# Differential attention: queries and keys reach the array's rows by transfers through DRAM instead of by products

## The chip, the cores and the metric

The kernel runs on one core of one Trainium2 chip. The metric is device microseconds of one execution, the median of several runs. Five engines work beside each other: PE (TensorE; its weight loads are listed apart as PEld), DVE (VectorE), ACT (ScalarE), POOL (GpSimd), and SP, which here only issues transfers. Sixteen DMA engines move the data.

## The reference

Two layers of a diffusion backbone run over 256 latent tokens and 128 context tokens, d_model 1024. In each layer one projection w_in feeds three groups of heads: A, latent attention (MLA), 6 heads; B, neighbourhood attention, 6 heads; C, differential attention, 4 heads. The heads are joined, projected by w_out, and a SwiGLU feed-forward part follows. The change concerns group C. For each of its heads, cut to what matters:

```python
q_df = _rms_pairs(_heads(df_q, 4), g_df_q)      # 2 x 32 numbers per head and token
k_df = _rms_pairs(_heads(df_k, 4), g_df_k)
q_df = _rope_pairs(q_df, cos, sin)              # latent tokens only
k_df = _rope_pairs(k_df, cos, sin)
s1 = q[..., :32] @ k1.T * 32 ** -0.5            # keys: cached context, then latent
s2 = q[..., 32:] @ k2.T * 32 ** -0.5
p = softmax(s1) - lam * softmax(s2)
o = rms(p @ v, g_df_sub) * (1 - lam_init)
```

## The kernel before, in words

All 384 tokens are kept as three blocks of 128 (t = 0, 1 latent, t = 2 context). Products that need float32 exactness are made from a rounded high part and a low remainder: `mm3` (lines 357 to 359) adds three products hi x hi, hi x lo and lo x hi. Weights come by SP into a `raw` tile (lines 275, 312, 398 for w_mod), ACT rounds them (`wh`, line 285), DVE subtracts (`wl`, line 291).

For group C the same exactness is had in one product. A query of 32 numbers and a key of 32 numbers are spread over the 128 rows of the array, as four groups of 32 rows: the queries as high, low, low, high and the keys as high, high, low, low. One product of 128 rows then sums all four pairings. The tile of a head for that, `du[h]`, has two parts: `du[h][0]` (named `qu`) with the queries of all tokens for both maps, and `du[h][1]` (named `ku`) with the cached keys in front (columns 0 to 127) and the new keys behind.

The work of a layer's attention stage is a list of tasks (`add(engine, planned duration, function, after=..., take=..., frees=..., prio=...)`). A planner (class `Plan`) orders them once at build time: it runs a small model of the engines with the planned durations and priorities, tries 300 drawn variations of the priorities, and keeps the best. The order that it gives is each engine's program order, fixed; at run time an engine waits in it. Projections of w_in (`g1`), early w_out products and the w_mod products (line 408) stand in this list with low priority, between the heads' small steps. `take` names a buffer of a kind that must be free (`ROOM` tells how many there are).

The steps of group C before the change:

- `done_d(p)` for head pair p and block t: copy out of PSUM, mean square, root (POOL, lines 577 and 578), scaling, rotation into `dfo[p][:, t]` (tokens on partitions; 4 groups of query numbers, then 4 of keys). Block 2's keys are stored (line 1327).
- `df_unit(h)`: `fetch` (line 1351) brings the cached keys into `tok` by four transfers of 32 rows; `high` (ACT, line 1354) and `low` (DVE, line 1358) make their parts in `ku`. Then for each block t: `parts_hi` (ACT, lines 1371 and 1372) rounds the head's queries and keys into a `tok` tile, each twice; `parts_lo` (POOL, line 1377) makes the remainders; `stack` (PE, line 1384) multiplies four 128x128 arrangements of them with the identity `identr`, which transposes and spreads them at once; `queries` (ACT, line 1387) and `keys` (DVE, line 1390) copy the result from PSUM into `qu` and `ku`.
- `diff_step(h, t)`: scores (PE, line 1078), softmax, transposes of the probabilities (line 1045), output products (line 1425).

The other names in the rows below: line 1181 is the output product of a pair of heads of A or B, line 935 and 1255 are transposes of A and B, `bias` (line 1137) are B's bias tables, `vn` are B's values, `brief` a small work tile, `out_newc` the new caches that the kernel returns.

Of the kernel before, what the change touches and what calls it, by code (L numbers as in the profile page):

```python
# [12 lines left out]
F32 = mybir.dt.float32  # L13
F32R = mybir.dt.float32r
# [4 lines left out]
P = 128  # L19
DM = 1024  # L20
KD = DM // P
NT = 384
# [39 lines left out]
ROOM = {'z': 3, 's': 2, 't': 2, 'raw': 3, 'graw': 2, 'w': 3, 'tok': 4, 'brief': 2, 'row': 5, 'un': 3, 'e': 4, 'pT': 3, 'pd': 2, 'bias': 2}  # L62
# [151 lines left out]
def trunk(ctx: ExitStack, tc, xT_d, cv_d, crow_d, pcol_d, prow_d, cache_d, dfk_d, rope_d, bias_d, ident_d,  # L214
# [10 lines left out]
    ps_m = ctx.enter_context(tc.tile_pool(name="ps_m", bufs=1, space=PSUM))  # L225

    cnt = [0]

    def nm(s):
        cnt[0] += 1  # L230
        return f"{s}_{cnt[0]}"
# [31 lines left out]
    identr = cst.tile([P, P], F32R, name="identr")  # L263
# [390 lines left out]
    for l in range(DEPTH):  # L654
# [86 lines left out]
        if l == 0:  # L741
            nst = {}
            add(ACT, 0.25, lambda: nc.scalar.activation(sv[:, :, 0:2], cv, AF.Silu), ready=5.0, prio=2 * URGENT)
            add(ACT, 0.2, lambda: nc.scalar.activation(identr, ident, AF.Copy), ready=20.0)
# [538 lines left out]
        dfo, vd, df_ready, vd_ready = {}, [], [{}, {}], [[], []]  # L1283

        def done_d(p):
            hd = slice(2 * p, 2 * p + 2)

            def done(t, z, unit, room):
# [18 lines left out]
                def rotate():  # L1307
                    if p not in dfo:
                        dfo[p] = ws.tile([P, 3, 8, 32], F32, name=nm("dfo"))
                    n, o = (v.rearrange("p (i h) d -> p i h d", i=2) for v in (heads(x["n"], 8), dfo[p][:, t]))  # L1310
# [3 lines left out]
                    if t < 2:  # L1314
# [8 lines left out]
                        nc.vector.tensor_tensor(dfo[p][:, t], dfo[p][:, t], tmp, op=ALU.add)  # L1323
                    else:
                        nc.vector.tensor_tensor(o, n, each(prow[:, PR_DQ:PR_DQ + 64].rearrange("p (i d) -> p i d", i=2)), op=ALU.mult)
                    if t == 2:
                        nc.sync.dma_start(new_d[l, :, CA_DFK + P * p:CA_DFK + P * p + P], dfo[p][:, t, 4:8, :].rearrange("p h d -> p (h d)"))
# [9 lines left out]
                df_ready[p][t] = add(DVE, 1.35 if t < 2 else 0.42, rotate, after=[e], frees=[a], prio=pr)  # L1337
# [4 lines left out]
        def df_unit(h, after, pr):  # L1342


            y = {}

            def fetch():
                du[h] = units(2, P, F32R)
                y["kc"] = tok(256).rearrange("p (a t) -> p a t", a=2)
                for i in range(4):  # L1350
                    nc.sync.dma_start(y["kc"][32 * i:32 * i + 32], dfk_d[l, :, 2 * h:2 * h + 2, :])

            def high():
                nc.scalar.activation(du[h][1][:, :, 0:P], y["kc"], AF.Copy)

            def low():
                kd = du[h][1]
                nc.vector.tensor_tensor(kd[64:, :, 0:P], y["kc"][64:], kd[64:, :, 0:P].bitcast(F32), op=ALU.subtract)
            a = add(DMA, 0.5, fetch, after=after, take=("tok",), prio=pr)
            b = add(ACT, 0.31, high, after=[a], prio=pr)  # L1360
            out = [add(DVE, 0.34, low, after=[b], frees=[a], prio=pr)]
            for t in range(3):
                x = {}

                def parts_hi(t=t, x=x):
                    src = dfo[h // 2][:, t].rearrange("p (i a) d -> p i a d", i=2)[:, :, 2 * (h % 2):2 * (h % 2) + 2, :]
                    both = tok(576, F32R)
                    x["st"] = [v.rearrange("p (a s d) -> p a s d", a=2, d=32) for v in (both[:, :320], both[:, 320:])]
                    x["sb"] = [src[:, i].unsqueeze(2).to_broadcast([P, 2, 2, 32]) for i in range(2)]
                    for i in range(2):  # L1370
                        nc.scalar.activation(x["st"][i][:, :, 0:2, :], x["sb"][i], AF.Copy)
                    nc.scalar.activation(x["st"][0][:, :, 4, :], src[:, 0], AF.Copy)

                def parts_lo(x=x):
                    for i in range(2):
                        st = x["st"][i]
                        nc.gpsimd.tensor_tensor(st[:, :, 2:4, :], x["sb"][i], st[:, :, 0:2, :].bitcast(F32), op=ALU.subtract)

                def stack(tag, x=x):
                    x["pt"] = pt = acc(tag).rearrange("p (i a t) -> p i a t", i=2, a=2)  # L1380
                    for i in range(2):
                        for a in range(2):
                            w = x["st"][i][:, a, 1 - i:5 - i, :].rearrange("p s d -> p (s d)")
                            nc.tensor.matmul(pt[:, i, a, :], w, identr, start=True, stop=True)

                def queries(t=t, x=x):
                    nc.scalar.activation(du[h][0][:, :, t * P:(t + 1) * P], x["pt"][:, 0], AF.Copy)

                def keys(t=t, x=x):
                    nc.vector.tensor_copy(du[h][1][:, :, KEY0[t]:KEY0[t] + P], x["pt"][:, 1])  # L1390
                c = add(ACT, 0.56, parts_hi, after=[a, df_ready[h // 2][t]], take=("tok",), prio=pr)
                d = add(POOL, 0.98, parts_lo, after=[c], prio=pr)
                e = add(PE, 0.47, stack, after=[d], take=("t",), frees=[c], prio=pr)
                out.append(add(ACT, 0.27, queries, after=[e], frees=[e], prio=pr))
                out.append(add(DVE, 0.34, keys, after=[e], frees=[e], prio=pr))
            return out

# [409 lines left out]
```

## Time and profile before

| what | value |
|---|---|
| median of 3 runs | 1011.09 us (1009.39 to 1011.51) |
| profiled execution | 1011.29 us, its span 1009.5 us, clock 0.998 |
| attention stage of layer 0 | about 60 to 215 us of the span |
| attention stage of layer 1 | about 545 to 700 us |
| weights and caches read | 159.69 MB from HBM; 3.05 MB written |

The span runs from the first to the last instruction of the profiled execution. Rows of PE give matmuls whose ends are modelled; rows of PEld give the weight loads, which overlap them. A row of a group lists line, engine, operation, tiles (written <- read), shape, count, then busy time, mean ns of one, and the idle time of the engine just before with what ended it. Lines 357 to 359 with `z` are projections.

### The profile page before, as it was taken

How to read it: one execution, taken by the hardware profiler on the slowest of the kernel's cores; microseconds unless marked ns; L12 is line 12 of the kernel's file. 1: busy time of each engine (PE TensorE's matmuls, PEld its weight loads, DVE VectorE, ACT ScalarE, POOL GpSimd, SP SyncE). 2: the span in 40 equal slices, each digit the busy share in tenths (PEclk: the TensorE clock that was granted, in tenths of full speed). 3: DMA queues.
4: the chain of work that ended last, by engine and by line, in shares of the span. 5: the costliest groups of instructions: out<-in, count | busy, mean ns of one | idle time of the engine just before them, and what ended most of it. 6: DMA issues, size and time to landing. Idle time of an engine off the chain costs nothing.

```text
span 1009.5 us, 16623 instructions
## 1 busy us (share of the span) xinstructions
PE 995.5 (99%) x6074; PEld 929.6 (92%) x6074; DVE 721.8 (71%) x1637; ACT 512.6 (51%) x1206; POOL 174.4 (17%) x263
## 2 busy tenths in 40 slices
PE   9999999999999999999999999999999999999998
PEld 8877778899999999999978878888999999999998
DVE  4678778887999999964356887788889655554342
ACT  3466778765433333333326778796553433333221
POOL 2166123201000000100015633240010000000000
PEclk9999999999999999999999999999999999999999
DMA  9865643327575757684462143322574525244451
GB/s 361 329 200 180 193 135 125 108 87 255 186 242 186 240 181 225 188 278 136 126 216 96 48 152 90 106 89 82 195 243 148 165 88 163 85 127 123 131 146 37
DMA packets 128209, 163.82 MB, mean 162 GB/s; under 512 B 5120, under 2 KB 107136, under 8 KB 125824
## 3 DMA queue, kind: packets, MB, share of 16 engines
q1 hardware_dynamic: 119712, 134.33, 41.5%
q0 software_dynamic: 6832, 27.77, 7.9%
q8 instruction: 48, 0.79, 0.3%
q10 hardware_dynamic: 1584, 0.66, 0.2%
q14 instruction: 33, 0.27, 0.1%
HBM read 159.69 MB, written 3.05 MB: 161 GB/s over the span
## 4 chain that ended last, share of the span: by engine, by line
PE 89%; ACT 5%; DVE 2%; POOL 1%; DMA 1%; issue 1%; ACTq 0%; DVEq 0%; POOLq 0%
PE z L357 13%; PE z L359 13%; PE z L358 13%; PE t L358 6%; PE t L357 6%; PE t L359 6%; PE s L357 5%; PE s L358 5%; PE s L359 5%; PE s L1078 4%; PE t L1045 2%; PE m L408 2%; PE t L1181 1%; PE s L952 1%; PE s L750 1%
## 5 line engine op out<-in xcount | busy, mean ns | idle before, releaser
L285 ACT ACTIVATE wh<-raw 128x768 fp32r<-128x768 f32 (+3 forms) x224 | 203.5, 909 | 365.4 <-PE z L358 138.1
L291 DVE TENSOR_TENSOR wl<-raw,wh 128x768 fp32r<-128x768 f32 (+3 forms) x224 | 231.8, 1035 | 112.5 <-ACT wh L285 110.9
L357 PE MATMUL z<-fh,wh 128*128 128x386 f32 x304 | 103.2, 339 | 0.0
L358 PE MATMUL z<-fl,wh 128*128 128x386 f32 x304 | 103.1, 339 | 0.0
L357 PE MATMUL z<-wh,hh 128*128 128x384 f32 (+1 forms) x264 | 101.3, 384 | 1.8 <-ACT hh L550 1.4
L359 PE MATMUL z<-fh,wl 128*128 128x386 f32 x304 | 102.6, 338 | 0.0
L480 DVE CUSTOM_DVE_ANT_0 sums<-wt,sums,pcol 128x1024 f32<-128x1024 f32 x80 | 102.3, 1278 | 0.3 <-ACT sums L469 0.3
L359 PE MATMUL z<-wh,hl 128*128 128x384 f32 (+1 forms) x264 | 90.5, 343 | 0.5 <-DVE hl L558 0.5
L358 PE MATMUL z<-wl,hh 128*128 128x384 f32 (+1 forms) x264 | 90.0, 341 | 0.0
L578 POOL TENSOR_TENSOR small<-small,mhalf 128x4 f32<-128x4 f32 (+4 forms) x58 | 75.5, 1302 | 4.8
L357 PE MATMUL s<-fh,wh 128*128 128x386 f32 x200 | 68.2, 341 | 0.0
L357 PE MATMUL t<-fh,wh 128*128 128x386 f32 x200 | 68.1, 340 | 0.0
L358 PE MATMUL t<-fl,wh 128*128 128x386 f32 x200 | 67.8, 339 | 0.0
L358 PE MATMUL s<-fl,wh 128*128 128x386 f32 x200 | 67.7, 339 | 0.0
L359 PE MATMUL s<-fh,wl 128*128 128x386 f32 x200 | 67.5, 338 | 0.0
L359 PE MATMUL t<-fh,wl 128*128 128x386 f32 x200 | 67.5, 338 | 0.0
L1101 ACT ACTIVATE e<-s,small 128x384 f32<-128x384 f32 (+1 forms) x114 | 57.8, 513 | 15.2 <-DVE small L1090 9.0
L474 POOL DMA_DIRECT2D wt<-in_w_modT x40 | 21.5, 539 | 252.4 <-DVE mod L480 186.5
L357 PEld LDWEIGHTS z<-wh,hh 128*128 128x128 f32 x264 | 50.0, 189 | 11.0 <-issue 4.6
L358 PEld LDWEIGHTS z<-fl,wh 128*128 128x128 f32 x304 | 57.5, 189 | 0.0
L359 PEld LDWEIGHTS z<-fh,wl 128*128 128x128 f32 x304 | 57.3, 189 | 0.0
L357 PEld LDWEIGHTS z<-fh,wh 128*128 128x128 f32 x304 | 57.2, 188 | 0.0
(299 smaller groups left out, 2414.4 us busy)
## 6 DMA issues: line engine op xcount, KB each, us to landing
raw<-in_w_gate SPq DMA_DIRECT2D x22, 1024.0 KB, 6.2
raw<-in_w_up SPq DMA_DIRECT2D x22, 1024.0 KB, 5.4
raw<-in_w_down SPq DMA_DIRECT2D x32, 704.0 KB, 4.7
wt<-in_w_modT POOLq DMA_DIRECT2D x40, 512.0 KB, 4.1
raw<-in_w_mod SPq DMA_DIRECT2D x16, 1024.0 KB, 5.1
raw<-in_w_in SPq DMA_DIRECT2D x40, 384.0 KB, 4.0
raw<-in_w_out SPq DMA_DIRECT2D x8, 640.0 KB, 4.4
qu<-in_w_mod SPq DMA_DIRECT2D x8, 512.0 KB, 8.5
```

Of the source, the lines that this page charges most:

```text
L285: nc.scalar.activation(hi, src, AF.Copy)
L291: nc.vector.tensor_tensor(lo, src, hi.bitcast(F32), op=ALU.subtract)
L357: nc.tensor.matmul(out, sh, mh, start=first, stop=False)
L358: nc.tensor.matmul(out, sh, ml, start=False, stop=False)
L359: nc.tensor.matmul(out, sl, mh, start=False, stop=last)
L408: nc.tensor.matmul(self.pm[32 * g:32 * g + 32, :n], sv[:, kb + k, :], w[g // self.per][:, k, i * n:(i + 1) * n], start=(kb + k == 0), stop ...
L474: nc.gpsimd.dma_start(self.w[:, self.loaded % 3], w_modT[l, c * P:(c + 1) * P])
L480: nc.vector.tensor_tensor_reduce(self.junk, self.w[:, self.n % 3], self.s[:, v], 1.0, pcol[l][:, PC_BMOD + c:PC_BMOD + c + 1], ALU.mult, A ...
L578: nc.gpsimd.tensor_tensor(out, t[:, :n], mhalf[:, :n], op=ALU.pow)
L1045: nc.tensor.transpose(pt[:, b, :], x, ident)
L1078: nc.tensor.matmul(ps[:, i, :], q, k, start=True, stop=True)
L1101: nc.scalar.activation(x["e"][i], ps[:, j, :], AF.Exp, bias=x["mx"][:, i:i + 1], scale=-1.0 if bias else 1.0, accum_out=x["su"][:, i:i + 1])
```

## The change

`done_d` goes further than before. After the rotation, which now writes a tile `dfo` of one pair and block, the four query groups (128 columns) and the four key groups (128 columns) are each transposed once (`turn`, two transposes on PE). `high` (ACT) rounds the transposed 128x256 from PSUM into a tile `hs`, `low` (DVE) subtracts to get the remainders, and `away` writes both, 128 partitions x 512 numbers, to a tile in DRAM, `parts_d[p]`, of which block t is a third. `df_unit(h)` no longer has `parts_hi`, `parts_lo`, `stack`, `queries` and `keys`. It keeps the cached keys as they were, and a step `spread` issues eight transfers on SP, four for the queries and four for the keys: each reads the high or the low part of one head, 2 x 32 rows of 384 tokens, from DRAM and writes it to 32 rows of `qu` or `ku`. It comes after the `fetch` of the head and after the stores of all three blocks of its pair. The planner's durations are 0.7 (`away`) and 2.3 (`spread`), and transfers get its usual 2.8 on top until their data count as there.

```diff
-ROOM = {..., 'pd': 2, 'bias': 2}
+ROOM = {..., 'pd': 2, 'bias': 2, 'dfo': 2, 'hs': 2}
...
+        parts_d = [dram.tile([P, 2, 2, NT], F32, tag=f"parts{p}", name=nm("parts")) for p in range(2)]
...
-                    if p not in dfo:
-                        dfo[p] = ws.tile([P, 3, 8, 32], F32, name=nm("dfo"))
+                    x["o"] = wk.tile([P, 8, 32], F32, tag="dfo", name=nm("dfo"), bufs=ROOM["dfo"])
...
+                def turn(tag):
+                    x["pt"] = acc(tag)[:, :256].rearrange("p (i t) -> p i t", i=2)
+                    for i in range(2):
+                        nc.tensor.transpose(x["pt"][:, i, :], x["o"][:, 4 * i:4 * i + 4, :].rearrange("p h d -> p (h d)"), ident)
+
+                def high():
+                    x["hs"] = wk.tile([P, 2, 2, P], F32R, tag="hs", name=nm("hs"), bufs=ROOM["hs"])
+                    nc.scalar.activation(x["hs"][:, 0], x["pt"], AF.Copy)
+
+                def low():
+                    nc.vector.tensor_tensor(x["hs"][:, 1], x["pt"], x["hs"][:, 0].bitcast(F32), op=ALU.subtract)
+
+                def away():
+                    nc.sync.dma_start(parts_d[p][:, :, :, t * P:(t + 1) * P], x["hs"].bitcast(F32))
...
-                df_ready[p][t] = add(DVE, 1.35 if t < 2 else 0.42, rotate, after=[e], frees=[a], prio=pr)
+                f = add(DVE, 1.35 if t < 2 else 0.42, rotate, after=[e], take=("dfo",), frees=[a], prio=pr)
+                if t == 2:
+                    add(DMA, 0.3, store, after=[f], frees=[f], prio=pr)
+                g = add(PE, 0.23, turn, after=[f], take=("t",), frees=[f], prio=pr)
+                u = add(ACT, 0.3, high, after=[g], take=("hs",), frees=[g], prio=pr)
+                v = add(DVE, 0.33, low, after=[u], frees=[g], prio=pr)
+                df_ready[p][t] = add(DMA, 0.7, away, after=[v], frees=[u], prio=pr)
...
+            def spread():
+                src = parts_d[h // 2][64 * (h % 2):64 * (h % 2) + 64]
+                for i, order in enumerate(((0, 1, 1, 0), (0, 0, 1, 1))):
+                    for j, w in enumerate(order):
+                        nc.sync.dma_start(du[h][i][32 * j:32 * j + 32, :, (0, P)[i]:(0, P)[i] + NT].bitcast(F32),
+                                          src[:, w, i].rearrange("(a r) t -> r a t", a=2))
...
-                c = add(ACT, 0.56, parts_hi, after=[a, df_ready[h // 2][t]], take=("tok",), prio=pr)
-                d = add(POOL, 0.98, parts_lo, after=[c], prio=pr)
-                e = add(PE, 0.47, stack, after=[d], take=("t",), frees=[c], prio=pr)
-                out.append(add(ACT, 0.27, queries, after=[e], frees=[e], prio=pr))
-                out.append(add(DVE, 0.34, keys, after=[e], frees=[e], prio=pr))
+            c = add(DVE, 0.34, low, after=[b], frees=[a], prio=pr)
+            d = add(DMA, 2.3, spread, after=[a] + [df_ready[h // 2][t] for t in range(3)], prio=pr)
+            return [c, d]
```

The planner orders the new list anew. Three places in layer 0 show what moved (the changed kernel's line numbers are up to 3 lower; 1333 is `turn`, 1337 the new `high`, 1343 `away`, 1373 `fetch`, 1387 `spread`).

First, PE where the last scores of the third MLA pair are done and head 1 is made ready. Before (1384 is the stack, 1714 the tiles of a pair of B, `z` a projection):

```order
L1078 MATMUL s_1892<-ku_640,qu_639 128x384
L1078 MATMUL s_1897<-ku_640,qu_639 128x128 x2
L1045 MATMUL t_1902<-ident,e_1846 128x128 x3
L1045 MATMUL t_1915<-ident,e_1880 128x128 x3
L408 MATMUL m_1699<-raw_1729,sv 32x256 x8
L1384 MATMUL t_1936<-identr,tok_1830 128x128 x4
L1045 MATMUL t_1947<-ident,e_1920 128x128 x3
L1078 MATMUL s_1952<-ku_1714,qu_1713 128x384
L1384 MATMUL t_1960<-identr,tok_1867 128x128 x4
```

Now, from the same last scores on:

```order
L1077 MATMUL s_1920<-ku_661,qu_660 128x128 x2
L1044 MATMUL t_1925<-ident,e_1874 128x128 x3
L1180 MATMUL t_1931<-pT_1560,vm_133 64x256
L1180 MATMUL t_1931<-pT_1613,vm_133 64x256
...
L357 MATMUL z_1734<-wh_1798,hh_120 128x384
L358 MATMUL z_1734<-wl_1815,hh_120 128x384
L359 MATMUL z_1734<-wh_1798,hl_121 128x384
L1077 MATMUL s_2105<-ku_1946,qu_1945 128x384
L1077 MATMUL s_2107<-ku_1946,qu_1945 128x384
```

The stacks are gone, and head 1's first two scores (`ku_1946`, `qu_1945`) stand 46 rows behind the last MLA score, with no PE work for the head itself between.

Second, SP at the same place. Before (the four `tok` transfers are head 1's cached keys):

```order
L1219 DMA ku_1714<-in_cache 128x3x128
L398 DMA raw_1729<-in_w_mod 128x2x1024
L1250 DMA out_newc<-brief_1850 128x128
L1351 DMA tok_1908<-in_dfk 32x256 x4
L398 DMA raw_1945<-in_w_mod 128x2x1024
L1137 DMA bias_1997<-in_bias 128x640
```

Now:

```order
L312 DMA raw_1860<-in_w_in 128x768 x2
L398 DMA raw_1895<-in_w_mod 128x2x1024
L1373 DMA tok_1947<-in_dfk 32x256 x4
L1387 DMA qu_1945<-parts_136 32x2x384 x4
L1387 DMA ku_1946<-parts_136 32x2x384 x4
L1136 DMA bias_2034<-in_bias 128x640
```

Behind the four transfers of the cached keys stand the eight of `spread`; the bias tables and the next w_mod load come behind them.

Third, PE where a pair's blocks are turned, some 160 rows ahead of head 0's first score. This piece is new:

```order
L1333 MATMUL t_942<-ident,dfo_903 128x128 x2
L408 MATMUL m_703<-raw_846,sv 32x512 x4
L951 MATMUL s_961<-qu_512,ku_513 128x288 x2
L934 MATMUL t_968<-ident,tok_820 96x128 x3
L994 MATMUL s_975<-ku_513,ckT_130 128x384
L934 MATMUL t_980<-ident,tok_820 96x128 x3
L951 MATMUL s_988<-qu_512,ku_513 128x288 x2
L951 MATMUL s_1009<-qu_512,ku_513 128x288 x2
L1333 MATMUL t_1019<-ident,dfo_1007 128x128 x2
```

The turns of blocks 1 and 2 stand among MLA's own products, in the time in which before no C work stood on PE.

More of the change, by code (lines that the diff above doesn't have):

```diff
@@ L61 @@
 HOPS = {('pe', 'act'): 0.22, ('pe', 'dve'): 0.22, ('act', 'pe'): 0.22, ('dve', 'pe'): 0.27, ('pool', 'dve'): 0.18, ('dve', 'pool'): 0.18, ('act', 'dve'): 0.15, ('dve', 'act'): 0.13}
-ROOM = {'z': 3, 's': 2, 't': 2, 'raw': 3, 'graw': 2, 'w': 3, 'tok': 4, 'brief': 2, 'row': 5, 'un': 3, 'e': 4, 'pT': 3, 'pd': 2, 'bias': 2}
+ROOM = {'z': 3, 's': 2, 't': 2, 'raw': 3, 'graw': 2, 'w': 3, 'tok': 4, 'brief': 2, 'row': 5, 'un': 3, 'e': 4, 'pT': 3, 'pd': 2, 'bias': 2, 'dfo': 2, 'hs': 2}
 CHUNKS = (((0, 416),),) + tuple(tuple((c + 128 * p, 128) for c in (1568, 1824, 2080)) for p in range(2)) + tuple(
@@ L225, in trunk @@
     ps_m = ctx.enter_context(tc.tile_pool(name="ps_m", bufs=1, space=PSUM))
+    dram = ctx.enter_context(tc.tile_pool(name="dram", bufs=1, space=bass.MemoryType.DRAM))
     cnt = [0]
@@ L262, in trunk @@
     nc.gpsimd.dma_start(ident, ident_d)
-    identr = cst.tile([P, P], F32R, name="identr")
     rope = cst.tile([P, 2, 2, 32], F32, name="rope")
@@ L743, in trunk @@
             add(ACT, 0.25, lambda: nc.scalar.activation(sv[:, :, 0:2], cv, AF.Silu), ready=5.0, prio=2 * URGENT)
-            add(ACT, 0.2, lambda: nc.scalar.activation(identr, ident, AF.Copy), ready=20.0)
             def idle(n, *tag):
@@ L1280, in done_n @@
             return done
-        dfo, vd, df_ready, vd_ready = {}, [], [{}, {}], [[], []]
+        vd, df_ready, vd_ready = [], [{}, {}], [[], []]
+        parts_d = [dram.tile([P, 2, 2, NT], F32, tag=f"parts{p}", name=nm("parts")) for p in range(2)]
         def done_d(p):
@@ L1307, in rotate @@
                 def rotate():
-                    if p not in dfo:
-                        dfo[p] = ws.tile([P, 3, 8, 32], F32, name=nm("dfo"))
-                    n, o = (v.rearrange("p (i h) d -> p i h d", i=2) for v in (heads(x["n"], 8), dfo[p][:, t]))
+                    x["o"] = wk.tile([P, 8, 32], F32, tag="dfo", name=nm("dfo"), bufs=ROOM["dfo"])
+                    n, o = (v.rearrange("p (i h) d -> p i h d", i=2) for v in (heads(x["n"], 8), x["o"]))
                     def each(g):
@@ L1322, in rotate, with store @@
                                                         c4[:, :, s, :].unsqueeze(1).to_broadcast([P, 4, 2, 8]), op=ALU.mult)
-                        nc.vector.tensor_tensor(dfo[p][:, t], dfo[p][:, t], tmp, op=ALU.add)
+                        nc.vector.tensor_tensor(x["o"], x["o"], tmp, op=ALU.add)
                     else:
                         nc.vector.tensor_tensor(o, n, each(prow[:, PR_DQ:PR_DQ + 64].rearrange("p (i d) -> p i d", i=2)), op=ALU.mult)
-                    if t == 2:
-                        nc.sync.dma_start(new_d[l, :, CA_DFK + P * p:CA_DFK + P * p + P], dfo[p][:, t, 4:8, :].rearrange("p h d -> p (h d)"))
+                def store():
+                    nc.sync.dma_start(new_d[l, :, CA_DFK + P * p:CA_DFK + P * p + P], x["o"][:, 4:8, :].rearrange("p h d -> p (h d)"))
+                def turn(tag):
[9 more added lines that the diff above has]
+                    nc.sync.dma_start(parts_d[p][:, :, :, t * P:(t + 1) * P], x["hs"].bitcast(F32))
                 pr = PDD
@@ L1359, in df_unit @@
             a = add(DMA, 0.5, fetch, after=after, take=("tok",), prio=pr)
             b = add(ACT, 0.31, high, after=[a], prio=pr)
[L1361 to L1390, printed above, removed]
-                c = add(ACT, 0.56, parts_hi, after=[a, df_ready[h // 2][t]], take=("tok",), prio=pr)
-                d = add(POOL, 0.98, parts_lo, after=[c], prio=pr)
-                e = add(PE, 0.47, stack, after=[d], take=("t",), frees=[c], prio=pr)
-                out.append(add(ACT, 0.27, queries, after=[e], frees=[e], prio=pr))
-                out.append(add(DVE, 0.34, keys, after=[e], frees=[e], prio=pr))
@@ L1396, in df_unit @@
-            return out
+            c = add(DVE, 0.34, low, after=[b], frees=[a], prio=pr)
+            d = add(DMA, 2.3, spread, after=[a] + [df_ready[h // 2][t] for t in range(3)], prio=pr)
+            return [c, d]
         dn = {}
```

## The prediction

> **What bounds the kernel now.** I read the page first: the busy shares and the chain that ended last.
>
> ```profile
> span 1009.5 us, 16623 instructions
> PE 995.5 (99%) x6074; PEld 929.6 (92%) x6074; DVE 721.8 (71%) x1637; ACT 512.6 (51%) x1206; POOL 174.4 (17%) x263
> ...
> PE 89%; ACT 5%; DVE 2%; POOL 1%; DMA 1%; issue 1%; ACTq 0%; DVEq 0%; POOLq 0%
> ```
>
> PE is busy nearly throughout and carries 89% of the chain. That is a mean over stages, so I cut the span into the two attention stages (60 to 215 us in layer 0, 545 to 700 us in layer 1), where every edited instruction lies, and the feed-forward stages behind them.
>
> ```profile
> core 0: us, PE busy (x) PEld busy (x) DVE busy (x) ACT busy (x) POOL busy (x), PEclk, DMA share, GB/s
> 60.00:215.00 155.00, 152.18 (x988) 123.12 (x989) 124.31 (x354) 113.63 (x357) 56.20 (x78) 1.00 0.43 139
> 215.00:518.00 303.00, 303.00 (x1727) 301.65 (x1726) 238.48 (x450) 121.94 (x188) 22.08 (x39) 1.00 0.62 200
> 545.00:700.00 155.00, 152.63 (x951) 131.68 (x951) 127.97 (x354) 120.49 (x379) 61.47 (x86) 1.00 0.31 98
> ```
>
> In the attention stages PE is idle for 155 - 152.18 = 2.8 us and 155 - 152.63 = 2.4 us, DVE for some 30 us, ACT for some 38 us, and the DMA engines work less than half of the time. The projections of w_in, and behind them those of w_out, stand between the heads as filler. So PE work that is taken out here should shorten the stage by nearly its own time. Only what a new wait costs has to come off.
>
> **The change, part by part.** *PE.* Removed are the stacks: 4 heads x 3 blocks x 4 products = 48 in each layer, 24 groups of four in all. Added are 3 blocks x 2 head pairs = 6 turns in each layer, 12 in all, of two 128x128 transposes each. A stack, a pair of transposes and the score behind them stand one after the other in the timeline of the weight loads:
>
> ```profile
> 137.94 0.52 PEld L1384 LDWEIGHTS t<-identr,tok 128*128 128x128 f32 x4 [0.61 <-issue]
> 138.41 0.20 PEld L1045 LDWEIGHTS t<-ident,e 128*128 128x128 f32 x2
> 138.58 0.30 PEld L1078 LDWEIGHTS s<-ku,qu 128*128 128x128 f32 x2
> ```
>
> From start to start the four products take 138.41 - 137.94 = 0.47 us, and to the end of their loads 0.52 us. Two transposes take 138.58 - 138.41 = 0.17 us, or 0.20 us to the end. I take 0.50 and 0.20 us: 24 x 0.50 = 12.0 us go and 12 x 0.20 = 2.4 us come, a net 9.6 us. The bounds are 24 x 0.47 - 12 x 0.22 = 8.6 us (a turn somewhat longer than the row) and 24 x 0.52 - 12 x 0.17 = 10.4 us. All of it lies in stages where PE is the bound, so all of it is on the path.
>
> *ACT, DVE, POOL.* The groups of the first attention stage, layer 1 being the same within 2%:
>
> ```profile
> L1377 POOL TENSOR_TENSOR tok<-dfo,tok 128x128 fp32r<-128x128 f32 x24 | 12.2, 536 | 5.3 <-ACT tok L1371 5.3
> L1371 ACT ACTIVATE tok<-dfo 128x128 fp32r<-128x128 f32 x24 | 6.1, 304 | 0.8 <-POOL tok L1377 0.8
> L1390 DVE CAST ku<-t 128x256 fp32r<-128x256 f32 x12 | 5.1, 421 | 2.4 <-ACT qu L1387 1.4 <-PE t L1384 0.8
> L1387 ACT ACTIVATE qu<-t 128x256 fp32r<-128x256 f32 x12 | 4.6, 381 | 2.2 <-PE t L1384 1.6 <-DVE ku L1390 0.4
> L1372 ACT ACTIVATE tok<-dfo 128x64 fp32r<-128x64 f32 x12 | 3.0, 248 | 0.0
> L1358 DVE TENSOR_TENSOR ku<-tok,ku 64x256 fp32r<-64x256 f32 x4 | 1.7, 424 | 0.1
> ```
>
> ACT loses 6.1 + 3.0 + 4.6 = 13.7 us in each layer and gains six roundings of 128x256 out of PSUM, priced by L1387: 6 x 0.38 = 2.3 us. DVE loses 5.1 us and gains six subtractions, nearest in form to L1358: 6 x 0.42 = 2.5 us. POOL loses 12.2 us and gains nothing. None of these engines is the bound (table above), so I cost and credit them at nothing; PE's own work is the cover. What their relief could give at most is PE's idle time, 2.8 + 2.4 = 5.2 us. The rounding of the identity that is dropped runs once and on an idle ACT: nothing.
>
> *Transfers.* Each turn's parts go to DRAM in one transfer of 128 x 2 KB = 256 KB, six in a layer. Each head then reads eight pieces of 32 rows x 2 x 384 floats = 96 KB, 32 in a layer, 3.1 MB. Together that is 4.7 MB in each layer beside 139 GB/s x 155 us = 21.5 MB; the DMA share goes from 0.43 to about 0.52, so bandwidth is no bound. The trace has no such piece. Its neighbours, of the same stage:
>
> ```profile
> raw<-in_w_in SPq DMA_DIRECT2D x10, 384.0 KB, 3.8
> bias<-in_bias SPq DMA_DIRECT2D x4, 320.0 KB, 3.0
> tok<-in_dfk SPq DMA_DIRECT2D x16, 32.0 KB, 3.8
> out_newc<-dfo SPq DMA_DIRECT2D x2, 64.0 KB, 1.6
> ```
>
> ```profile
> L1351 SPq DMA_DIRECT2D tok<-in_dfk x32: 326/417/1250, 81.9 to 655.4; - x32
> DMA to landing us min/median/max: 1.6/2.3/4.9
> ```
>
> A store of 256 KB lands after something between the 1.6 us of a 64 KB store and the 3.8 us of a 384 KB load; I take 2.5 us. The pieces are nearest to the four in_dfk pieces, which also write 32 rows each: 0.42 us to issue, 1.6 to 4.9 us to land. From the moment a head's tiles are free, SP issues 4 pieces of in_dfk and 8 of the parts: 12 x 0.42 = 5.0 us, and the last lands 1.6 to 4.9 us later: 6.6 to 9.9 us. I take 7.3, with the median of 2.3. The 38 new issues of a layer cost SP 38 x 0.42 = 16 us of 155.
>
> *What hides that.* The least cover I find in the order is that of head 1 in layer 0. Its tiles come free with the last MLA score of 128 columns (L1077 s_1920 in the order), and its own first score stands 46 rows behind. Between lie two pair outputs, four scores of 384 columns, a w_mod group, 18 projection products and 20 transposes. Prices from the chain, and from 303.00 us over 1727 products in the second row of the table of stages (0.175 us each):
>
> ```profile
> 137.30 0.65 PE s L1078 x2
> ...
> 143.64 1.45 PE t L1181 x12
> ...
> 146.19 1.00 PE m L408 x16
> ```
>
> 2 x 1.45 + 4 x 0.65 + 1.00 + 18 x 0.175 + 20 x 0.10 = 11.7 us of cover against 6.6 to 9.9. In layer 1 head 0's score stands behind a good 20 us of such rows after its last turn. So I cost the waits at 0 to 2 us in all, the value taken 0.5 us, because cover exceeds even the slow landing. If a head is late, the projections behind its score on PE stand with it, since PE's queue is in order.
>
> *Sum.* The profiled execution took 1011.3 us (span 1009.5 and 1.8 around it), 0.2 above the median of 1011.1. 1011.3 - 9.6 + 0.5 = 1002.2; against the median 1002.0.
>
> [...]
>
> **Rivals.** *The stages are paced by the softmax chains, not by PE.* For it: ACT and DVE hold 7% of the whole chain though PE is called 99% busy, and PE's loads leave 32 and 23 us of the two stages open. Against it: the idle rows of PE, and the filler. If half of the removed work only turns into idle PE, the time is 1011.1 - 4.8 = 1006.3. If all of it does, the time stays at 1011.
>
> *More is gained than PE's work.* In layer 0 the first stack waits for POOL:
>
> ```profile
> POOL tok L1377 <- ACT tok L1371: 30.8, 9, 8.0
> ...
> 93.17 1.29 POOL tok L1377 x2
> ```
>
> The chain passes through that subtraction (second row) before the first stacks. With it gone, and ACT relieved of 11 us in each layer, up to the 5.2 us of PE's idle time could go too: 1011.1 - 9.6 - 2.6 = 998.9 with half of it.
>
> *Slower: head-of-line blocking on SP.* The chain of a head begins on SP behind weight loads that stand until a buffer is split:
>
> ```profile
> SPq L312 <- DVE wl L291: 27.9, 7, 6.0
> ```
>
> In layer 0 a w_mod load stands directly ahead of head 1's transfers, in layer 1 w_in loads stand ahead of two heads. If such a wait of 6.0 us falls between the freeing of a head's tiles and its transfers, 7.3 + 6.0 = 13.3 us meet a cover of 11.7, and with the slow landing 15.9, so PE stands for 1.6 to 4.2 us. It takes more than 9.6 + 2.0 = 11.6 us over the eight heads to be slower, 1.5 us on each. At a mean of 1.6 us on each, 12.8 us, the time is 1011.1 + 3.2 = 1014. Against it: the wait of 6.0 us is the longest of seven, and the other heads have more cover. *That the stacks stay* is excluded: the order has no row of them left.
>
> **How the numbers follow.** The full PE gain with small waits (about 1002; 999.8 to 1004.5): 0.60. Half of it eaten by chains or late transfers (about 1006; 1004.5 to 1009): 0.19. More than PE's work (996.5 to 999.8): 0.10. Gain wholly turned to waits, within 0.2% (2 us, about what a measurement can tell from no change): 0.04. Slower: 0.07. So faster 0.89, same 0.04, slower 0.07. The range leaves out the slower and unchanged cases and the outer half of the other two: 998 to 1008.
>
> **What the profile after would show.** PE with some 48 - 12 = 36 fewer instructions in each stage and each stage shorter by 4 to 5 us; POOL's row 24 us smaller and ACT's 23 us; no idle time of PE or PEld before the scores L1077 that ends with a DMA into qu or ku; pieces of parts landing within 5 us. I am wrong if PE idles in front of a head's first score, if SP waits for the store of the parts with weight loads behind it that ACT then waits for, or if the stages shrink by less than 3 us while PE's idle time grows.

## The result and the profile after

| | median | range, runs |
|---|---|---|
| before, beside it | 1011.34 us | 1009.39 to 1014.73, 6 |
| after | 1003.92 us | 999.48 to 1005.07, 6 |
| ratio | 0.9917 | 95%: 0.9898 to 0.9935 |

The ratio is worth 8.4 us (6.6 to 10.3). The forecast was 1002.0, within 998 to 1008. The profiled execution of the changed kernel took 1003.3 us. Its page and its stages, in the rows that were shown of before, with the first 60 us added; the columns are again the width of the stage, busy time and count of PE, PEld, DVE, ACT and POOL, the granted clock, the DMA share and GB/s:

```profile
span 1001.5 us, 16414 instructions
PE 987.9 (99%) x6002; PEld 921.1 (92%) x6002; DVE 711.6 (71%) x1625; ACT 495.8 (50%) x1121; POOL 150.6 (15%) x215
...
PE 79%; DVE 1%; ACT 0%; issue 0%; POOL 0%; DVEq 0%
```

```profile
0.00:60.00 60.00, 54.36 (x507) 47.38 (x508) 30.67 (x102) 23.30 (x55) 14.55 (x24) 0.91 0.85 311
60.00:215.00 155.00, 153.40 (x984) 122.69 (x984) 122.61 (x355) 110.18 (x335) 48.15 (x60) 1.00 0.57 176
545.00:700.00 155.00, 154.92 (x957) 134.01 (x956) 126.20 (x357) 115.51 (x346) 46.22 (x62) 1.00 0.42 128
```

PE makes 72 products fewer (6074 to 6002), and POOL's row is 23.8 us smaller. The chain can't be set beside that of before: its shares add up to 80%, since it goes back only to 187 us of the span, and most of layer 0's attention lies ahead of that. PE's idle time in the two attention stages went from 2.8 and 2.4 us to 155 - 153.40 = 1.6 and 155 - 154.92 = 0.1 us. The surprise is the first row: in the first 60 us, where the change has no instruction, PE is idle for 5.6 us and its clock is 0.91 on average. The same 60 us of before, with 2.2 us of idle time and the full clock:

```profile
0.00:60.00 60.00, 57.83 (x546) 50.68 (x546) 34.58 (x110) 29.35 (x77) 14.80 (x31) 1.00 0.88 329
```

How the gain lies in the two layers is read from two marks in PE's timeline: the start of the first product that makes MLA's keys (line 995, after 994), and the start of the first feed-forward product behind the attention stage (`z<-fh,wh`). Before, then after:

```profile
55.73 0.81 PE L995 MATMUL s<-ku,ckT 128*128 128x384 f32 x2
...
235.42 0.34 PE L357 MATMUL z<-fh,wh 128*128 128x386 f32 x1
...
537.22 2.54 PE L995 MATMUL s<-ku,ckT 128*128 128x384 f32 x4
724.74 0.33 PE L357 MATMUL z<-fh,wh 128*128 128x386 f32 x1
```

```profile
59.44 1.46 PE L994 MATMUL s<-ku,ckT 128*128 128x384 f32 x4
236.70 0.34 PE L357 MATMUL z<-fh,wh 128*128 128x386 f32 x1
...
537.26 1.53 PE L994 MATMUL s<-ku,ckT 128*128 128x384 f32 x4 [0.71 <-PE z L359]
716.45 0.34 PE L357 MATMUL z<-fh,wh 128*128 128x386 f32 x1
```

Layer 0's attention, from mark to mark, took 179.7 us before and takes 177.3 now, 2.4 less, and the first mark is reached 3.7 us later: at 236.7 us the changed kernel is behind. Layer 1's took 187.5 and takes 179.2, 8.3 less. The forecast had 4 to 5 us in each.

The marks don't bound the same work in layer 0. Ahead of the first one PE made 520 products before and makes 505 now: 12 projections of 416 columns and 3 transposes have moved behind it. At 0.19 us from one such projection to the next in the kernel before, and 0.10 us for a transpose, I estimate them at 2.6 us. For the same work layer 0's stage is thus some 5 us shorter, as forecast, and its start some 6 us longer. In layer 1 nothing but the change crossed the marks (1125 products, now 1089); some 1 us of its 8.3 is the clock, which in before was 0.50 from 536.0 to 539.4 us, so that the four products at the mark took 2.54 us against 1.53. All this is read from one execution of each kernel, and l0_only below, with the same order in layer 0, took 179.5 us from mark to mark: the split is good to some 2 us.

That left four questions: what layer 0 lost at its start, whether PE's products are the price at all or the relief of ACT, DVE and POOL, whether the transfers are really covered, and what the new order does by itself.

### The profile page after: what moved, and what is told of

The parts are those of the page before. It is cut to its first block, busy times and chain, and to the rows that moved or that the text cites. A ratio compares the mean times of both kernels' runs of the same rounds, so it can differ in the third digit from the quotient of the medians.

```text
span 1001.5 us, 16414 instructions
## 1 busy us (share of the span) xinstructions
PE 987.9 (99%) x6002; PEld 921.1 (92%) x6002; DVE 711.6 (71%) x1625; ACT 495.8 (50%) x1121; POOL 150.6 (15%) x215
## 4 chain that ended last, share of the span: by engine, by line
PE 79%; DVE 1%; ACT 0%; issue 0%; POOL 0%; DVEq 0%
PE z L357 12%; PE z L358 12%; PE z L359 12%; PE t L358 6%; PE t L357 6%; PE t L359 6%; PE s L358 5%; PE s L357 5%; PE s L359 5%; PE s L1077 2%; PE t L1044 2%; PE t L1180 1%; PE t L1422 1%; PE s L951 1%; PE s L994 1%; PE m L408 0%
```

## The experiments

Ratios are to the kernel before on the same chip, so kernels that ran on different chips are compared by ratios; 0.001 is 1.0 us. "The planner" is the one that writes the order when the kernel is built.

### One layer at a time

The changed steps in layer 1 alone and in layer 0 alone; the order of PE in the changed layer is that of the changed kernel, in the other that of before.

```diff
+        stacked = l == 0        # l1_only; l == 1 in l0_only
...
-                    if p not in dfo:
-                        dfo[p] = ws.tile([P, 3, 8, 32], F32, name=nm("dfo"))
+                    if stacked:
+                        if p not in dfo:
+                            dfo[p] = ws.tile([P, 3, 8, 32], F32, name=nm("dfo"))
+                        x["o"] = dfo[p][:, t]
+                    else:
+                        x["o"] = wk.tile([P, 8, 32], F32, tag="dfo", name=nm("dfo"), bufs=ROOM["dfo"])
...
+                if stacked:
+                    df_ready[p][t] = add(DVE, 1.35 if t < 2 else 0.42, rotate, after=[e], frees=[a], prio=pr)
+                    return
```

> The change in layer 1 alone; layer 0 keeps the stacks and has the order of before word for word, layer 1 has the order of after word for word. Theory A (PE's removed work shortens each attention stage, and a reordered start of layer 0 takes part of it back): layer 1 gave 8.3 us in the profiles (187.5 to 179.2 us from its first up-projection to its first feed-forward product), and no start is lost, so 1011.3 - 8.3 = 1003.0, no slower than the full change. Theory B (PE's work alone counts, the rest of layer 1's gain was chance of one profiled execution): half of 9.6, so 1006.5.

> The change in layer 0 alone; layer 1 keeps the stacks and the order of before. Theory A: the attention stage of layer 0 gains some 2.4 us and the reordered start loses 3.7 us, so about 1012.6, no gain at all. Theory C (each layer gains its PE work, 4.8 us, whatever the start): 1006.5.

Measured: l1_only 1003.29 us, ratio 0.9921 (0.9909 to 0.9934); l0_only 1012.22 us, ratio 1.0012 (0.9997 to 1.0027). Both are what theory A had. With its order, layer 1 alone brings 8.0 us, and layer 0 alone, its start included, nothing that can be told from zero. Together they make the whole change.

### What layer 0 lost at its start

The order shows that the new plan exchanged two neighbours on PE near the start: `total`, which sums the squares (line 770, 771 before), now stands ahead of the first products of w_mod. The timeline of after, without the products of w_mod (line 408) in between; the columns are start, duration, and in brackets the idle time ahead with what ended it:

```profile
12.88 0.83 PE L770 MATMUL t<-ones,sq 128*128 128x1 f32 x6 [2.29 <-DVE sq L762]
...
14.65 2.77 PE L749 MATMUL s<-ones 128*128 128x128 f32 x12
```

And of before:

```profile
12.63 0.83 PE L771 MATMUL t<-ones,sq 128*128 128x1 f32 x6
13.32 1.58 PE L750 MATMUL s<-ones 128*128 128x128 f32 x12
```

PE now stands for 2.29 us until DVE has the squares, and the products of w_mod, which in before began at 11.62 us, begin behind `total`, at 13.64 us. Twelve products of 128x128 then take 2.77 us instead of 1.58. Two kernels exchange the pair: after_swap puts it back as it was before, before_swap does the exchange in the kernel before.

```diff
+        if l == 0:                                  # before_swap
+            i, j = work.index(mod_task), work.index(tot_task)
+            work[i], work[j] = tot_task, mod_task
```

> The changed kernel with two neighbouring tasks of PE in layer 0 exchanged: the first w_mod products stand ahead of the product that sums the squares, as before the change. Theory A: PE no longer idles 2.3 us at 10.6 us of the span and the clock isn't halved after it; 3 to 4 us come back, so about 1000.4. Theory D (the shortfall of layer 0 is the transfers' contention with the weight loads; the start is noise): 1003.9, no change from after within 1 us.

> The kernel before with the same two tasks exchanged the other way: the product that sums the squares stands ahead of the first w_mod products. Nothing else is changed. Theory A: PE idles some 2 us before it and the clock is halved in windows behind, so 3 to 4 us slower than before, about 1014.8. Theory D: no change, 1011.3 within 1 us.

Measured: after_swap 1002.00 us, ratio 0.9917 (0.9903 to 0.9932); before_swap 1013.33 us, ratio 1.0020 (1.0009 to 1.0030). In the kernel before the exchange costs 2.0 us, less than the 3.5 that I expected, with an idle time of 1.6 us in place of 2.3 and no half clock behind it. In the changed kernel putting it back shortens the profiled span from 1001.5 to 999.0 us, but the ratio is the changed kernel's own: neither theory A's 3 to 4 us nor theory D's nothing is settled there.

A second wait stands some 12 us behind, and the exchange doesn't touch it. The first projection in after, and then the 7 us from 25 us on, in after and in before:

```profile
25.23 0.71 PE L357 MATMUL z<-wh,hh 128*128 128x416 f32 x1 [2.12 <-ACT hh L550]
```

```profile
25.00:32.00 7.00, 6.58 (x44) 4.94 (x45) 2.88 (x5) 1.24 (x3) 0.00 (x0) 0.51 0.66 227
```

```profile
25.00:32.00 7.00, 7.00 (x66) 6.48 (x66) 6.57 (x31) 3.54 (x6) 1.23 (x2) 1.00 1.03 405
```

PE waits 2.1 us for the rounded input of the projections, which in before came in time, and then runs at half clock, 0.51 over these 7 us. after_swap has the same wait of 2.1 us, and over the same 7 us its clock is 0.76 on average, which is worth 3.4 us at half clock. So the start of the changed kernel has two waits and some 10 us at half clock (0.50 from 14.86 to 18.27 us and from 25.10 to 31.92 us), and after_swap takes away only the larger part of the first wait (0.8 us is left) and the half clock behind that (its clock is 1.00 from 10 to 25 us). No run takes the second wait away by itself, so its price isn't shown. In after_seed2 below, whose order has no such wait in layer 0 and whose clock is 1.000 over its whole span, the first mark comes at 56.77 us instead of 59.44, with 21 products more ahead of it.

### Are PE's products the price?

before_thin takes products away from the kernel before and touches nothing else, the order least of all. pe_back gives the changed kernel as much PE work as the change took from it.

```diff
-                    for i in range(2):                             # before_thin, in stack()
-                        for a in range(2):
-                            w = x["st"][i][:, a, 1 - i:5 - i, :].rearrange("p s d -> p (s d)")
-                            nc.tensor.matmul(pt[:, i, a, :], w, identr, start=True, stop=True)
+                    w = x["st"][0][:, 0, 1:5, :].rearrange("p s d -> p (s d)")
+                    nc.tensor.matmul(pt[:, 0, 0, :], w, identr, start=True, stop=True)
...
-                    for i in range(2):                             # pe_back, in turn()
+                    for i in 5 * (0, 1):
```

> The kernel before, its orders untouched, with one edit: each of the 24 stacks makes one of its four products, and the copies to the queries and keys write that one to all the places. It leaves out three of four products of the stacks, and the values with them; every copy, wait and buffer stays. TensorE loses 24 x 3 products of about 0.125 us, 9.0 us, close to the 9.6 us that the change takes away, and nothing else of the change is there: no round trip by way of DRAM, no relief of ScalarE, VectorE and GpSimd, no new order. Theory A (TensorE's instructions are the whole price, in both layers): 1002.5 us, half of it in each layer. Theory R (the gain of the change came in part from the relief of ScalarE, VectorE or GpSimd, or from the new order of the second layer): about 1006.5 us. Theory S (the softmax's chains pace the scores): 1009 us or more.

> The changed kernel, with the product that sums the squares put back behind the first product of the modulation's weights in the first layer, and each turn of a head's channels issuing its two transposes five times over. This gives TensorE 96 more transposes of about 0.10 us, 9.6 us (8.2 to 10.5), which is what the change took from it; the transfers, the copies of ScalarE and VectorE and the order stay as in the changed kernel. Theory A (TensorE's instructions are the whole price): 1002.0 + 9.6 = 1011.6 us. Theory R (the gain came in part from the relief of ScalarE, VectorE or GpSimd, whose copies stay away here): about 1006.5 us.

Measured: pe_back 1012.97 us, ratio 1.0020 (1.0009 to 1.0031), 0.0103 or 10.4 us above after_swap's ratio: theory A. But before_thin: 1010.24 us, ratio 0.9994 (0.9984 to 1.0005). Products priced at 9 us were gone, and the 0.6 us gained can't be told from nothing: theory A fails there, and theory S stands. The page of before_thin shows PE's busy row 6.5 us smaller and the span all but the same; PE's idle time went from 14.0 to 19.6 us:

```profile
span 1008.6 us, 16480 instructions
PE 989.0 (98%) x6002; PEld 919.1 (91%) x6002; DVE 721.4 (72%) x1637; ACT 512.0 (51%) x1206; POOL 174.8 (17%) x263
```

Where it went is seen at the first stacks of layer 0 (the first of two is shown). PE's timeline of before, and then of before_thin:

```profile
94.09 0.84 PE L1384 MATMUL t<-identr,tok 128*128 128x128 f32 x4
...
96.66 1.06 PE L408 MATMUL m<-raw,sv 128*32 128x512 f32 x8
98.71 0.91 PE L1078 MATMUL s<-ku,qu 96*128 96x384 f32 x2 [0.99 <-ACT e L1101]
```

```profile
94.25 0.22 PE L1382 MATMUL t<-identr,tok 128*128 128x128 f32 x1
...
96.20 1.06 PE L408 MATMUL m<-raw,sv 128*32 128x512 f32 x8
98.86 0.91 PE L1078 MATMUL s<-ku,qu 96*128 96x384 f32 x2 [1.59 <-ACT e L1101]
```

PE is 0.46 us earlier at the w_mod products (96.66 to 96.20), and then waits 1.59 us instead of 0.99 for ACT's exponential, so that the next scores start no earlier. The order had put those stacks where a softmax needed time. That leaves two readings: with another order the work would pay (P), or ACT, DVE and POOL hold the stage in any order (R). Two kernels tell them apart. thin_plan is before_thin with the planner told that a stack is short. lean_plan keeps 96 PE instructions in the stacks and drops the work of ACT and POOL ahead of them.

```diff
-                e = add(PE, 0.47, stack, after=[d], take=("t",), frees=[c], prio=pr)
+                e = add(PE, 0.12, stack, after=[d], take=("t",), frees=[c], prio=pr)     # thin_plan
...
-                            w = x["st"][i][:, a, 1 - i:5 - i, :].rearrange("p s d -> p (s d)")
-                            nc.tensor.matmul(pt[:, i, a, :], w, identr, start=True, stop=True)
+                            w = dfo[h // 2][:, t, 4 * i:4 * i + 4, :].rearrange("p h d -> p (h d)")     # lean_plan
+                            nc.tensor.transpose(pt[:, i, a, :], w, ident)
...
-                c = add(ACT, 0.56, parts_hi, after=[a, df_ready[h // 2][t]], take=("tok",), prio=pr)
-                d = add(POOL, 0.98, parts_lo, after=[c], prio=pr)
-                e = add(PE, 0.47, stack, after=[d], take=("t",), frees=[c], prio=pr)
+                e = add(PE, 0.47, stack, after=[a, df_ready[h // 2][t]], take=("t",), prio=pr)
```

> The kernel before with one of the four products in each of the 24 stacks, as in before_thin, and now the planner's cost of a stack goes from 0.47 to 0.12, so that the planner writes a new order for all engines. Three of four products of the stacks are left out, and their values with them; the copies of ScalarE and VectorE and GpSimd's subtractions are all there. before_thin took the same 9 us of products out of the old order and gained 1 us: TensorE came sooner to products that still waited for others. Theory P (TensorE's work is the price, but only in an order that is written for it): 1001 to 1005 us. Theory R (ScalarE, VectorE and GpSimd hold the scores' stretch too, so that their relief is needed whatever the order): 1007 us or more.

> The kernel before with TensorE's 96 products of the stacks kept, as 96 transposes that read the rotated channels directly; ScalarE's copies of the high parts and GpSimd's subtractions, 13 us and 24 us of work, are left out, and with them the split into parts. The queries' and keys' copies of ScalarE and VectorE stay, no transfer is added, and the planner writes a new order. In that order the sum of the squares stands ahead of the first product of the modulation's weights, which cost the changed kernel about 2 us. TensorE loses about 1.5 us, since a transpose is some 0.015 us shorter than a product of a stack. Theory P: 1011 to 1012 us. Theory R (relief of ScalarE and GpSimd gives the gain): 1007 us or less.

Measured: thin_plan 1004.64 us, ratio 0.9929 (0.9918 to 0.9941); lean_plan 1012.02 us, ratio 1.0002 (0.9993 to 1.0012). Both as theory P has it. The page of thin_plan, and then that of lean_plan:

```profile
span 1002.7 us, 16483 instructions
PE 986.1 (98%) x6002; PEld 919.7 (92%) x6002; DVE 718.9 (72%) x1637; ACT 510.5 (51%) x1206; POOL 172.0 (17%) x263
```

```profile
span 1010.3 us, 16430 instructions
PE 996.6 (99%) x6074; PEld 926.6 (92%) x6074; DVE 717.2 (71%) x1637; ACT 500.8 (50%) x1134; POOL 144.2 (14%) x215
```

thin_plan and before_thin have the same 6002 PE instructions and the same work on ACT, DVE and POOL; only the order is another, and the span is 5.9 us shorter. lean_plan has POOL's row lower by 30 us and ACT's by 12, and gains nothing. Both orders have the wait for the squares at the start, 1.75 us in thin_plan and 1.46 in lean_plan, which the exchange in before_swap priced at 2.0 us. Without it thin_plan would gain some 9 us, and lean_plan some 2, of which its shorter transposes are 1.5 by the estimate above. So PE's work is the price, but here it was paid out only by an order written for it; the relief of ACT and POOL is worth some 0.3 us by these figures, which are known to 1 or 1.5 us: nothing that can be measured.

### Are the transfers covered?

double_spread lets SP load each head's eight pieces twice, half_spread only the four of the keys.

```diff
-                for i, order in enumerate(((0, 1, 1, 0), (0, 0, 1, 1))):
+                for i, order in 2 * tuple(enumerate(((0, 1, 1, 0), (0, 0, 1, 1)))):                     # double_spread
+                for i, order in (0, (0, 1, 1, 0)), (1, (0, 0, 1, 1)), (1, (0, 0, 1, 1)):                # half_spread
```

> The changed kernel, with the product that sums the squares put back behind the first product of the modulation's weights in the first layer, and each head's eight pieces loaded from DRAM twice, the second load into the same place behind the first. A head's chain from the turn to the last piece gets longer by eight issues of 0.42 us and one landing of about 2.8 us, some 6 us, and 6.3 MB more are moved. Theory A (the transfers are covered by the scores of the head ahead, with 11.7 us at the least place against 7.3 us): 1002 to 1003 us, with waits at one head of the first layer at most. Theory T (the transfers' chain stands on the path already): 6 us at each of several heads, 1005 us or more, with TensorE's scores waiting for the pieces' transfers.

> As double_spread, with only the four pieces of the keys loaded a second time: four more issues on SyncE and 48 x 8 KB more for each head, half of what double_spread added. There the first load of the modulation's weights left SyncE 4.1 us later, TensorE waited 6.1 us for it, and 20 us were lost in all, while no score waited for a piece. Theory S (SyncE's queue behind the pieces has some 2 us of slack at each head): 1002 to 1005 us. Theory N (it has none, so that each issue more is paid in full): half of 20 us, 1010 to 1013 us.

Measured: double_spread 1022.13 us, ratio 1.0115 (1.0100 to 1.0131), 20 us above after_swap's ratio; half_spread 1014.78 us, ratio 1.0040 (1.0026 to 1.0054), 12 us above, a little more than theory N had. So there is no slack. But the place isn't the one that theory T named. PE's waits in double_spread, and the same line in half_spread:

```profile
PE m L408 <- DMA raw<-in_w_mod: 15.7, 4, 6.1
```

```profile
PE m L408 <- DMA raw<-in_w_mod: 6.5, 3, 2.7
```

In after_swap this line has 0.4 us. In double_spread four w_mod groups wait for their own weights, and behind the longest of these waits the group's eight products took 1.94 us, where the same group takes 1.06 us in after_swap, and the next six scores 2.01 us against 1.26. The mean granted clock of this execution is 0.993, that of after_swap's 0.998; from that I estimate the loss to the clock at 0.005 x 1020 = some 5 us. With the 15.3 us that the waits grew by this is about the 20 us. No score waited for a piece in either kernel. (The profiled execution of half_spread is its quickest, 1010.5 us; its span is 9.7 us above after_swap's, 6.1 of them these waits. The rest goes with the clock: its mean is 0.994 against 0.998, some 4 us over the span by the same estimate.) SP's issues behind a head of layer 0 in after_swap (first piece at 92.88), and then in double_spread (93.29):

```profile
92.88 1.79 SPq L1389 DMA_DIRECT2D qu<-parts  x4
...
97.57 0.35 SPq L398 DMA_DIRECT2D raw<-in_w_mod  x1
```

```profile
93.29 1.79 SPq L1389 DMA_DIRECT2D qu<-parts  x4
...
98.00 1.75 SPq L1389 DMA_DIRECT2D qu<-parts  x4
99.89 1.75 SPq L1389 DMA_DIRECT2D ku<-parts  x4
101.74 0.37 SPq L398 DMA_DIRECT2D raw<-in_w_mod  x1
```

A w_mod load of 1 MB stands right behind the pieces on SP. Measured from the first piece it leaves 4.69 us later in after_swap and 8.45 in double_spread, 3.8 us more, and its product starts 8.4 us behind it (110.12 us), where in after_swap 6.0 us were enough (103.54 us). So at this head the later issue is the larger part of PE's wait of 6.1 us, and a slower landing the rest. Issues and traffic grew together in both kernels, so what each is worth in all was not told apart. In the changed kernel PE waits for w_mod loads in `raw` for 0.2 us in all: the eight pieces just fit, and ahead of those loads the queue has no time left.

### What an order is worth

The same two kernels, with the planner's random draws started from another number; both have `total` behind the first w_mod products.

```diff
-        draw = random.Random(0)
+        draw = random.Random(1)      # before_seed1; Random(2) in after_seed2
```

> The kernel before, with the planner's search started from another random number; all the work is the same, in another order. The first products of the modulation's weights stand ahead of the sum of the squares, as in the kernel before. It measures what the order alone moves. Theory P: 1011 us, some 3 us to either side; an order that is worth 6 us or more would put the second layer's gain down to the order.

> The changed kernel, with the planner's search started from another random number; all the work is the same, in another order, and the first products of the modulation's weights stand ahead of the sum of the squares. Theory P: 1001 us, some 3 us to either side, so that it stays under every order of the kernel before; if the gain was the luck of one order: 1007 us or more.

Measured: before_seed1 1013.33 us, ratio 1.0016 (1.0005 to 1.0028); after_seed2 1001.88 us, ratio 0.9906 (0.9892 to 0.9921). Another order moved each kernel by 1 to 2 us; the gap between the two is 8 us in the first pair of orders and 11 in the second. The marks of after_seed2:

```profile
56.77 1.46 PE L994 MATMUL s<-ku,ckT 128*128 128x384 f32 x4
231.84 0.34 PE L357 MATMUL z<-fh,wh 128*128 128x386 f32 x1
...
532.64 1.45 PE L994 MATMUL s<-ku,ckT 128*128 128x384 f32 x4
715.30 0.34 PE L357 MATMUL z<-fh,wh 128*128 128x386 f32 x1
```

Layer 0's attention takes 175.1 us here and layer 1's 182.7: 4.6 and 4.8 less than before. Here 6 projections moved ahead of the first mark, by the same estimate some 1 us, so that for the same work layer 0's stage is 3.6 us shorter and its start as long as before. The 8.3 us of layer 1 and the loss at the start of layer 0 were thus those of one order, not a property of the change. after_swap and after_seed2, about 2 us under the changed kernel by their medians, are the quickest versions run, and not clearly apart from each other or from it.

## Why the prediction was right, step by step

- *PE's price, a net 9.6 us: held.* The 96 products of the stacks are gone and 24 transposes came. Three kernels price that work on the path: 7.2 us for 9.0 taken away (thin_plan), 10.4 for 9.6 given back (pe_back), 8.4 for the whole change. Of these pe_back shows only what such work costs in an order with hardly a wait in it, not what its removal gives.
- *"All of it is on the path": right for the new order, wrong as it was argued.* The argument was that PE idles for 2.8 and 2.4 us only, and that projections stand as filler. before_thin refutes that: idle time shows the waits that are left in an order, not those that stand ready when a product goes. There the rival of the softmax chains holds: of the 6.5 us that left PE's busy row, 5.6 came back as idle time. It does not hold for the change, because the planner ordered everything anew with the new durations. The prediction did not price that step at all; it is what the gain rests on.
- *ACT, DVE and POOL, credited at nothing: held* by lean_plan for ACT and POOL (ratio 1.0002). The rival of a gain beyond PE's work, 998.9 us, gets no support from their relief: the first row shown for it is POOL's own wait for ACT, and in front of the stacks PE's idle time that ended with POOL was 0.2 us in the whole kernel. DVE's relief was not tried alone. PE's idle time in layer 1's stage did go, from 2.4 to 0.1 us, as that rival has it, but in after_seed2 it is 2.1 us (155 - 152.86): it went with one order. Of the sizes, POOL's row fell by 23.8 us (24 forecast) and ACT's by 16.8 (23 forecast): the durations of ACT's activations add up to 562.3 us before and 537.0 after, some 25 us less, but the page, with 512.6 and 495.8 us, counts the time in which two instructions overlap once.
- *The prices of the new steps: held, but for landings.* In order below: the rounding (0.38 us forecast), the subtraction (0.42), a store's landing (2.5), and a piece's issue (0.42) and landing (2.3, at most 4.9). The medians of the landings are 0.4 and 0.5 us above the forecast, and the slowest piece, 5.8 us, is past the 5 us that was given as a sign. The DMA share rose by more than forecast, to 0.57 against 0.52 in layer 0's stage.

```profile
L1337 ACT ACTIVATE hs<-t 128x256 fp32r<-128x256 f32 x12 | 4.6, 382 | 5.1 <-PE t L1333 5.1
L1340 DVE TENSOR_TENSOR hs<-t,hs x12: 406/417/426, 66.1 to 608.6; 128x256 fp32r<-128x256 f32 x12
...
L1343 SPq DMA_DIRECT2D parts<-hs x12: 518/519/1304, 66.6 to 609.1; - x12
DMA to landing us min/median/max: 2.6/2.9/6.2
...
L1387 SPq DMA_DIRECT2D qu<-parts x32: 302/425/1290, 96.0 to 636.4; - x32
DMA to landing us min/median/max: 1.9/2.8/5.8
```

- *"No idle time of PE before the scores that ends with a DMA": held.* All that the scores (line 1077) waited for in the changed kernel, in us and times:

```profile
ACT e L1100: 1.9, 5
issue: 0.8, 3
DVE ku L1261: 0.3, 1
ACT pd L1416: 0.2, 1
```

- *The cover of 11.7 us: right for the scores, and the wrong place to look.* What I had worked out is what lies between a head's tiles and its first score on PE. In after, head 1's pieces leave SP from 141.4 to 147.8 us, and its first score starts at 154.8. That cover isn't safe in every order, either; in after_seed2:

```profile
PE s L1077 <- DMA ku<-parts: 1.2, 2, 0.8
```

Nearer is what lies behind the pieces on SP: a w_mod load that PE waits for. Of the three rivals the blocking of SP's queue was the one nearest to deciding, though by another road than the one I gave it: not a wait that comes ahead of the pieces, but the pieces' own issue time ahead of a weight load. Its price was not 1.5 us more on each head against some cover; four issues more on each head, with their traffic, cost 12 us, which is more than the change gives.
- *Each stage shorter by 4 to 5 us: right on average, and the nearness of the sum is in part luck.* From mark to mark 2.4 and 8.3 us were measured, and 4.6 and 4.8 in another order; for the same work some 5 and 8.3, and 3.6 and 4.8. The loss at the start of layer 0, some 6 us for the same work, was in no term: in the trace it lies with the two waits near the start and the half clock behind them. In the changed kernel it more than took back the 3.5 us that layer 1 gave beyond its 4.8, and what is left lies near the sum. Of the signs of being wrong, "stages shrink by less than 3 us while PE's idle time grows" came in part: layer 0's stage shrank by 2.4 us between its marks, but PE's idle time grew ahead of that stage, not in it.
- *A reading that was off without moving the sum.* Layer 1's groups are not all within 2% of layer 0's: the mean of line 1358, which priced the new subtraction, is 523 ns there against 424. The subtraction itself took 417.

## What to carry to other kernels

Work that was taken from a busy engine paid here only when the order was free to close the gap; in the fixed order it turned into waits for whatever stood beside it. So try the removal in the old order and in a new one before you trust either number. When a step becomes transfers, the cover to work out is not only the time until its own data are read: look at what stands behind it in the issuing queue. And when a planner writes a new order, read its whole difference, since it may move things far from the edit, and start it from a few numbers before a gain is put down to one stage. Before two stages are compared between marks, count the work between them.

## What the hardware showed that I had not expected

After an idle time of 2.29 us PE ran at half clock. The stage of 15 to 18.3 us in after, and then in before_swap, where PE had idled for 1.6 us:

```profile
15.00:18.30 3.30, 3.30 (x14) 2.56 (x12) 0.58 (x3) 0.00 (x0) 0.00 (x0) 0.50 1.03 402
```

```profile
15.00:18.30 3.30, 3.30 (x50) 2.72 (x49) 1.40 (x4) 0.78 (x3) 0.00 (x0) 1.00 1.03 407
```

The granted clock, the third column from the right, is 0.50 for the whole of that stage in after and 1.00 in before_swap. So a wait can cost more than itself: the twelve products of 128x128 above took 1.2 us longer (2.77 against 1.58).

The stretch at 0.50 lasts 3.41 us there (14.86 to 18.27); the one behind the wait of 2.12 us for the projections' input lasts 6.82 us (25.10 to 31.92), and in before one of 3.41 us (535.98 to 539.39) comes behind a wait of 1.40 us. In l0_only the products of w_mod took 0.42 us each behind a wait of 1.17 us, and 0.28 in before; in double_spread a w_mod group took 1.94 us behind a wait of 6.08 us, and 1.06 in after_swap. But behind the 1.62 us of before_swap the clock stayed at 1.00 (to 32 us), and in half_spread a w_mod group took 1.07 us behind a wait of 2.35 us. So the length of a wait alone doesn't tell whether PE slows down behind it. What does was not shown; no run was made to test it.

The clock also goes with the spread of one kernel's executions: the ten of before_seed1 run from 1009.35 us at a mean clock of 1.000 to 1014.55 us at 0.994, more than the 1.6 us by which its order differs from that of before.
